# Mixer A's projection: moving operand in storage order, result permuted when it is split

## The chip, the cores and the metric

The kernel runs on one core of one Trainium2 chip. The metric is the device time of one execution in microseconds; lower is better. The engines are named as in the profile: PE (matrix multiply; PEld is its weight load), DVE (vector), ACT (scalar), POOL (GpSimd), SP (which here only issues DMAs). ACTq and POOLq are the queues on which ACT and POOL issue DMAs of their own.

## The reference

One decoder layer on 2048 tokens of width 1024. Cut to what matters here:

```python
h = rmsnorm(x, g_attn[l])
proj = jnp.einsum('bsd,de->bse', h, w_in[l]) + b_in[l]
qa, ka, va, qb, kb, vb = jnp.split(proj, splits, axis=-1)
oa = sliding_window_sink_gqa(qa, ka, va, sinks[l])   # Mixer A: rotary positions on q and k, window 128
ob = dilated_mixture(qb, kb, vb, rel_table)          # Mixer B: three dilated branches, T5 bias
mixed = jnp.concatenate([rmsnorm(oa, g_out_a[l]), rmsnorm(ob, g_out_b[l])], axis=-1)
x = x + jnp.einsum('bse,ed->bsd', mixed, w_o[l])
h = rmsnorm(x, g_ffn[l])
act = jax.nn.silu(h @ w_gate[l]) * (h @ w_up[l])
x = x + act @ w_down[l]
return rmsnorm(x, g_final)
```

Mixer A has 8 query heads and 2 key heads of 64 columns, so 512 + 128 columns of queries and keys; Mixer B has 8 and 8.

## The kernel before

Every fp32 product is made of three matmuls on operands split into a high and a low part (hh, hl for the normalised input, wh, wl for the weights). The input is held transposed: 128 partitions of the 1024 features in KC = 8 groups, by 2048 tokens (S). The tokens are stored by residue, token mod 16 first, in the order that the dilated branches of Mixer B want; four token tiles (t, NT = 4) of 512 columns make up the whole. Mixer A's attention wants another order, in which a block of 128 consecutive tokens lies together; in storage that is runs of 8 columns.

`project` has three stages. The first (to 148 us of the profiled execution) normalises x, transposes it into hh and hl and makes both mixers' values (`v_rows`). The second (148 to 280) makes Mixer A's queries and keys: five chunks c of 128 columns (0 to 3 queries, 4 keys), each with four tiles. `gemm(ps, w, t, True)` makes one tile of 24 matmuls of 128x512, whose moving operand is a view of hh or hl in Mixer A's order:

```python
mv = h[:, k, :].rearrange("p (r jj j a) -> p jj j r a", r=16, jj=4, j=4)[:, t]
```

A tile is then evicted with its rotary turn: DVE (L305) and ACT (L303) copy quarters with the halves exchanged, taking turns; DVE multiplies with cosine and sine (L307, L308); POOL adds (L309); ACT casts the high part (L311), DVE subtracts for the low part (L312), into a tile hia; SP stores it for two heads (`store_heads`, L185, 2 x 256 KB). The same stage makes Mixer B's bias tables, a step per tile: `rows(h)` multiplies a one-hot matrix to bias rows (accb), copies them out of the accumulator on ACT (lt) and stores them to a scratch Ls; `table(h)` loads them back skewed (tt, n4, n1), puts two parts in another order on DVE (L395, L396) and stores the table (Ts). Accumulators are eight.

The third stage (280 to 548) interleaves Mixer B's queries and keys (`proj_b`, 32 units of 24 matmuls with a contiguous moving operand, hi evicted by ACT L333 and DVE L334) with Mixer A's attention, `MixerA.unit`, which loads ka, va and qa (L534, L538, L542) on SP. Four B units come ahead of the first attention unit. `attend_b` follows; its first loads are q0 (L610) and the k tiles (L615).

A scheduler orders the instructions of each engine from this program; each engine then runs its own list in order and waits on semaphores. So what stands in an engine's queue behind a waiting instruction waits too, on SP and POOL as well.

Of the kernel before, what the change touches and what calls it, by code (L numbers as in the profile page):

```python
# [43 lines left out]
def shape_constants():  # L44
# [105 lines left out]
def project(tc, es, ident, half, x, g_attn, w_in, b_in, sinks, rel, rope, mask_a, onehot, sc):  # L150
# [19 lines left out]
    def gemm(ps, w, t, natural, tag="mm"):  # L170
        acc = ps.tile([P, 512], F32, tag=tag, name="acc")
        n = 0
        for k in range(KC):
            for a, h in ((w[0], hh), (w[0], hl), (w[1], hh)):
                if natural:
                    mv = h[:, k, :].rearrange("p (r jj j a) -> p jj j r a", r=16, jj=4, j=4)[:, t]
                else:
# [1 line left out]
                nc.tensor.matmul(acc, a[:, k, :], mv, start=(n == 0), stop=(n == 3 * KC - 1))  # L179
                n += 1  # L180
        return acc

    def store_heads(dst, h, hi, cols):
        for u in range(2):
            nc.sync.dma_start(dst[h + u].rearrange("s d n -> d s n")[:, :, cols], hi[u * 64:u * 64 + 64].bitcast(F32))  # L185
# [96 lines left out]
    with ExitStack() as ex:  # L282
        ps = ex.enter_context(tc.tile_pool(name="ps2", bufs=8, space=PSUM, reuse_waits="tile"))
        rp = ex.enter_context(tc.tile_pool(name="r1", bufs=2, reuse_waits="tile"))
# [9 lines left out]
        for c in range(5):  # L294
            w = load_w(c * P)
            for t in range(NT):
                cols = slice(t * 512, (t + 1) * 512)
                acc = gemm(ps, w, t, True)
                t1 = rp.tile([P, 512], F32, tag="t1", name="t1")
                for q4 in range(4):  # L300
                    d, s4 = t1[q4 * 32:(q4 + 1) * 32, :], acc[(q4 ^ 1) * 32:((q4 ^ 1) + 1) * 32, :]
                    if q4 % 2:
                        nc.scalar.copy(d, s4)  # L303
                    else:
                        nc.vector.tensor_copy(d, s4)  # L305
                t2 = rp.tile([P, 512], F32, tag="t2", name="t2")
                nc.vector.scalar_tensor_tensor(t2, acc, bcol[:, c:c + 1], tab[:, 0, cols], op0=ALU.add, op1=ALU.mult)  # L307
                nc.vector.scalar_tensor_tensor(t1, t1, bsw[:, c:c + 1], tab[:, 1, cols], op0=ALU.add, op1=ALU.mult)  # L308
                nc.gpsimd.tensor_add(t2, t2, t1)  # L309
                hi = rp.tile([P, 2, 512], F32R, tag="hi", name="hia")  # L310
                nc.scalar.copy(hi[:, 0], t2)  # L311
                nc.vector.tensor_sub(hi[:, 1], t2, hi[:, 0].bitcast(F32))  # L312
                store_heads(sc.qA if c < 4 else sc.kA, 2 * c if c < 4 else 0, hi, cols)
                n = c * NT + t - 2
                if 0 <= n < 2 * NH:
                    bias(n // NH, n % NH)
# [33 lines left out]
def bias_tables(tc, es, ps, rel, onehot, sc):  # L350
# [26 lines left out]
    def rows(h):  # L377
        lw = bw.tile([P, P], F32R, tag="lw", name="lw")
        nc.vector.tensor_scalar(out=lw, in0=ones, scalar1=rhi[:, h:h + 1].bitcast(F32), scalar2=None, op0=ALU.mult)
        lt = bw.tile([P, 3, 384], F32, tag="lt", name="lt")  # L380
        for b in range(3):
            acc = ps.tile([P, 384], F32, tag="mm", name="accb")
            nc.tensor.matmul(acc, lw, ohr[:, b, :], start=True, stop=True)
            nc.scalar.copy(lt[:, b, :], acc)
        nc.sync.dma_start(sc.L[h].rearrange("b p n -> p b n"), lt)

    def table(h):
# [7 lines left out]
        nc.vector.tensor_copy(tt[:, 128:384].rearrange("p (c i) -> p c i", c=4), n4.rearrange("p (i c) -> p c i", c=4))  # L395
        nc.vector.tensor_copy(tt[:, 384:640].rearrange("p (g c a) -> p g c a", g=4, c=4),  # L396
# [939 lines left out]
```

## Time and profile before

| | |
|---|---|
| median of 3 runs | 2397.68 us (2393.30 to 2399.03) |
| the profiled execution | 2399.05 us, its span 2397.3 us |
| mean granted TensorE clock | 0.98 |
| busy, share of the span | PE 96%, PEld 82%, DVE 67%, ACT 44%, POOL 21% |
| Mixer A's projection on PE | 147.8 to 279.8 us, 480 matmuls of 128x512 |
| B's projection and Mixer A's attention | 279.8 to about 548 us |

The rows in the prediction read: start or count, engine, line, operation, result<-operands by the program's names, shapes; behind a bar the busy time, the mean of one in ns, and the idle time ahead of it with what ended it.

### The profile page before, as it was taken

To read this page: it belongs to the slowest core of one execution; us is meant where nothing else is said; L and a number is where in the kernel's file an instruction comes from. 1 tells how busy PE (TensorE), PEld (TensorE's weight loads), DVE (VectorE), ACT (ScalarE), POOL (GpSimd) and SP (SyncE) were. 2 spreads that over 40 slices of the span, in tenths; PEclk is the share of its full clock that TensorE was granted. 3 is DMA by queue.
4 is the path that set the end of the run, shared out by engine and by line. 5 is a ranking of instruction groups with operands and counts; after the bars stand their busy time and mean duration, and the time that the engine had idled before them with its cause. 6 is when DMAs were issued, how large, how long until landed. Compare 5 with 4: busy or idle time off the path is not lost.

```text
span 2397.3 us, 34036 instructions
## 1 busy us (share of the span) xinstructions
PE 2302.2 (96%) x11765; PEld 1954.8 (82%) x11765; DVE 1608.9 (67%) x3155; ACT 1062.1 (44%) x2371; POOL 494.1 (21%) x447
## 2 busy tenths in 40 slices
PE   7999999997999979997999999899999999999998
PEld 7987788886999968885888888678888878888887
DVE  5435655456999986668877777787676747557555
ACT  5323355553988883434332323342333324444443
POOL 3211200001333220113233232423232330000000
PEclk9999999997999979998999999999999999999999
DMA  7666655559788566744554445333232339668663
GB/s 216 210 187 214 159 163 163 146 140 229 197 197 202 137 203 215 251 149 167 181 175 145 163 154 170 120 124 114 95 113 93 104 126 366 206 198 283 205 195 126
DMA packets 279228, 419.43 MB, mean 175 GB/s; under 512 B 24096, under 2 KB 152624, under 8 KB 274448
## 3 DMA queue, kind: packets, MB, share of 16 engines
q1 hardware_dynamic: 273072, 393.97, 53.9%
q10 hardware_dynamic: 3744, 17.11, 1.8%
q0 software_dynamic: 2240, 6.18, 1.0%
q8 instruction: 93, 1.52, 0.3%
q14 instruction: 79, 0.65, 0.1%
HBM read 278.11 MB, written 139.07 MB: 174 GB/s over the span
## 4 chain that ended last, share of the span: by engine, by line
PE 74%; DVE 11%; DMA 6%; ACT 4%; issue 3%; SPq 1%; POOL 1%; DVEq 0%; POOLq 0%; ACTq 0%
PE bY L1264 7%; PE acco L897 7%; PE Yu L1070 7%; PE acc L179 7%; PE Yg L1070 6%; PE bZ L1264 5%; PE bX L1264 5%; PE Zu L1070 5%; PE Xu L1070 4%; PE Zg L1070 4%; PE Xg L1070 4%; PE accv L246 4%; PE s L434 3%; DVE t L438 2%; PE pt L475 2%
## 5 line engine op out<-in xcount | busy, mean ns | idle before, releaser
L1217 DVE TENSOR_TENSOR o<-r,o 128x1024 fp32r<-128x1024 f32 x154 | 191.7, 1253 | 139.1 <-ACT o L1216 136.6
L1216 ACT CAST o<-r 128x1024 fp32r<-128x1024 f32 x154 | 161.3, 1050 | 227.9 <-PE bY L1264 84.0
L1164 POOL TENSOR_TENSOR c<-c,c 128x512 f32<-128x512 f32 x66 | 103.9, 1575 | 571.3 <-DVE c L1088 391.2
L1035 ACT CAST wh<-T 128x512 fp32r<-128x512 f32 x176 | 108.0, 623 | 248.1 <-PE Yu L1070 76.8
L456 ACT ACTIVATE p<-t,m 128x256 f32<-128x256 f32 (+1 forms) x384 | 179.0, 490 | 19.9 <-DVE m L682 19.7
L1264 PE MATMUL bY<-o 128*128 128x512 f32 x792 | 180.5, 389 | 0.0
L1264 PEld LDWEIGHTS bY<-o 128*128 128x128 f32 x792 | 148.6, 188 | 30.9
L179 PE MATMUL acc<-hh,wh 128*128 128x512 f32 x416 | 170.1, 409 | 0.7 <-DVE vt L249 0.7
L179 PE MATMUL acc<-hl,wh 128*128 128x512 f32 x416 | 170.2, 409 | 0.0
L179 PE MATMUL acc<-hh,wl 128*128 128x512 f32 x416 | 170.2, 409 | 0.0
L897 PE MATMUL acco<-woh,oT 128*128 128x512 f32 x512 | 164.0, 395 | 0.0
L481 DVE TENSOR_TENSOR hl<-pt,hl 128x512 fp32r<-128x512 f32 (+1 forms) x224 | 145.1, 657 | 22.0 <-ACT hl L480 21.5
L1037 DVE TENSOR_TENSOR wl<-T,wh 128x512 fp32r<-128x512 f32 x176 | 156.7, 901 | 0.4
L499 PE MATMUL o<-hl,v 128*128 128x128 f32 (+1 forms) x816 | 142.4, 299 | 10.6 <-DVE hl L481 7.4
L480 ACT CAST hl<-pt 128x512 fp32r<-128x512 f32 (+1 forms) x224 | 126.8, 574 | 38.8 <-PE pt L475 38.0
L475 PE MATMUL pt<-ident,p 128*128 128x128 f32 x848 | 135.5, 285 | 6.4 <-DVE hl L481 2.6
L434 PE MATMUL s<-k,q 128*128 128x256 f32 (+1 forms) x768 | 125.0, 299 | 16.6 <-DVE hl L481 6.2
L499 PEld LDWEIGHTS o<-hl,v 128*128 128x128 f32 x816 | 114.7, 200 | 14.4 <-DVE hl L481 9.8
L434 PEld LDWEIGHTS s<-k,q 128*128 128x128 f32 x768 | 106.0, 202 | 22.9 <-DVE hl L481 6.3
L1264 PE MATMUL bX<-o 128*128 128x512 f32 x528 | 120.6, 389 | 1.1 <-DVE o L1217 1.1
L1264 PE MATMUL bZ<-o 128*128 128x512 f32 x528 | 120.3, 389 | 0.0
L438 DVE CUSTOM_DVE_ANT_0 t<-s,tab 128x256 f32<-128x256 f32 (+1 forms) x344 | 112.6, 370 | 7.4 <-PE s L434 4.8
(470 smaller groups left out, 5817.4 us busy)
## 6 DMA issues: line engine op xcount, KB each, us to landing
r<-actS SPq DMA_DIRECT2D x154, 256.0 KB
actS<-c SPq DMA_DIRECT2D x128, 256.0 KB
wraw_g<-in_w_gate_dram SPq DMA_DIRECT2D x44, 512.0 KB
wraw_u<-in_w_up_dram SPq DMA_DIRECT2D x44, 512.0 KB
r<-wT SPq DMA_DIRECT2D x88, 256.0 KB
r<-in_w_down_dram SPq DMA_DIRECT2D x66, 256.0 KB
k<-kB SPq DMA_DIRECT2D x32, 512.0 KB
draw<-in_w_down_dram SPq DMA_DIRECT2D x22, 512.0 KB
```

The lines of the kernel that those rows point to most:

```text
L179: nc.tensor.matmul(acc, a[:, k, :], mv, start=(n == 0), stop=(n == 3 * KC - 1))
L434: nc.tensor.matmul(s[:, i, :n], b["q"], b["k"][m], start=(m == 0), stop=(m == 1))
L438: nc.vector.tensor_tensor_reduce(out=b["kv"](t[:, i, :n]), in0=b["kv"](s[:, i, :n]), in1=b["tab"], scale=-0.125, scalar=init, op0=ALU.add, ...
L456: nc.scalar.activation(b["pv"](p[:, i, :n]), b["tv"](b["t"]), AF.Exp, scale=-1.0, bias=nm[:, c:c + 1], accum_out=l[:, c:c + 1])
L475: nc.tensor.transpose(pt[:, sl, :], p[:, i, hfn * P:(hfn + 1) * P], ident)
L499: nc.tensor.matmul(out, v[:, vi, :], mov, start=(first and n == 1), stop=(last and n == 2 * len(jobs)))
L897: nc.tensor.matmul(acc, oT[t, g][kk // 2][:, kk % 2, a, i * P:(i + 1) * P], b[:, kk, :], start=(n == 0), stop=(n == 11))
L1037: nc.vector.tensor_sub(lo, src, hi.bitcast(F32))
L1070: nc.tensor.matmul(bank, a[:, k], b[:, k], start=(first and m == 0), stop=(m == 11), skip_group_check=not first)
L1216: nc.scalar.copy(o[:, 0], r)
L1217: V.tensor_sub(o[:, 1], r, o[:, 0].bitcast(F32))
L1264: nc.tensor.matmul(bank[i], o[:, u, 0, i * P:(i + 1) * P], o[:, v, 1, :], start=(first and j == 0 and m == 0), stop=(j == NP - 1 and m == ...
```

## The change

- hh and hl become four tiles each, one per token tile, and `gemm` reads the columns as they lie. The rope table's columns are put into the same order (in its host-made constant).
- Mixer A's result is brought into its order later: `rotated` evicts a tile up to the addition, `parted` casts and subtracts with writes in runs of 8 into one hia tile for a whole chunk, up to three tiles later, and stores 2 x 1 MB per chunk.
- The chunks run in the order 4, 0, 1, 2, 3; weights are loaded three tiles ahead, B's first weights before the stage ends.
- The bias tables go in finer steps: two of the 24 row pieces per tile, each with a store of its own; loads and the table's two copies on alternating tiles; the copies run on POOL.
- `proj_b` runs chunk 3 tile by tile, alternating queries and keys, and issues that chunk's 16 stores on ACT's queue.

The core of the diff (lines left out are the same edit at other places):

```diff
-    tok = (n // 128) * 128 + (n % 8) * 16 + res[(n % 128) // 8]
+    tok = (n % 128) * 16 + res[n // 128]
...
-    hh = cp.tile([P, KC, S], F32R, name="hh")
-    hl = cp.tile([P, KC, S], F32R, name="hl")
+    hh, hl = [], []
+    for t in range(NT):
+        hh.append(cp.tile([P, KC, 512], F32R, name=f"hh{t}"))
+        hl.append(cp.tile([P, KC, 512], F32R, name=f"hl{t}"))
...
-    def gemm(ps, w, t, natural, tag="mm"):
-                if natural:
-                    mv = h[:, k, :].rearrange("p (r jj j a) -> p jj j r a", r=16, jj=4, j=4)[:, t]
-                else:
-                    mv = h[:, k, t * 512:(t + 1) * 512]
-                nc.tensor.matmul(acc, a[:, k, :], mv, start=(n == 0), stop=(n == 3 * KC - 1))
+                nc.tensor.matmul(acc, a[:, k, :], h[t][:, k, :], start=(n == 0), stop=(n == 3 * KC - 1))
...
+    def store_heads(dst, h, hi, cols, q=nc.sync):
-            nc.sync.dma_start(dst[h + u].rearrange("s d n -> d s n")[:, :, cols], hi[u * 64:u * 64 + 64].bitcast(F32))
+            q.dma_start(dst[h + u].rearrange("s d n -> d s n")[:, :, cols], hi[u * 64:u * 64 + 64].bitcast(F32))
...
-        for c in range(5):
-            w = load_w(c * P)
...
+        rp = ex.enter_context(tc.tile_pool(name="r1", bufs=2, reuse_waits="tile"))
+        def rotated(c, t, w):
+            cols = slice(t * 512, (t + 1) * 512)
+            acc = gemm(ps, w, t)
...
+            t2 = rp.tile([P, 512], F32, tag="t2", name="t2", bufs=4)
...
+            nc.gpsimd.tensor_add(t2, t2, t1)
+            return t2.rearrange("p (r j a) -> p r j a", r=4, j=16)
+        def parted(c, t, t2):
+            if t == 0:
+                his[c] = rp.tile([P, 2, S], F32R, tag="hi", name="hia", bufs=1)
+            hi = his[c]
+            hj = [hi[:, u].rearrange("p (j r a) -> p r j a", j=16, r=16)[:, 4 * t:4 * t + 4] for u in range(2)]
+            tc.keep_in_program_order(nc.scalar.copy(hj[0], t2))
+            tc.keep_in_program_order(nc.vector.tensor_sub(hj[1], t2, hj[0].bitcast(F32)))
+            if t == NT - 1:
+                store_heads(sc.qA if c < 4 else sc.kA, 2 * c if c < 4 else 0, hi, slice(0, S))
+        his, behind, w = {}, [], {}
+        seq = [(c, t) for c in (4, 0, 1, 2, 3) for t in range(NT)]
+        w[4] = load_w(4 * P)
+        for n, (c, t) in enumerate(seq):
+            t2 = rotated(c, t, w[c])
+            if t == 1 and n + 3 < len(seq):
+                cn = seq[n + 3][0]
+                w[cn] = load_w(cn * P)
+            elif t == 1:
+                w_next = load_w(C_QB)
+            behind.append((c, t, t2))
+            if t in (0, 3):
+                for x_ in [x_ for x_ in behind if x_[1] in ((2, 3) if t == 0 else (0, 1))]:
+                    parted(*x_)
+                    del behind[[y[:2] for y in behind].index(x_[:2])]
+            if n >= 2:
+                bias(n - 2)
+        for x_ in behind:
+            parted(*x_)
...
+        w = {C_QB: w_next}
...
-                if t == 0:
-                    w = load_w(c0 + c * P)
+                if t == 0 and (c0, c) != (C_QB, 0):
+                    w[c0] = load_w(c0 + c * P)
...
-        units = [(c0, c, t) for c in range(4) for c0 in (C_QB, C_KB) for t in range(NT)]
+                store_heads(sc.kB if c0 == C_KB else sc.qB, 2 * c, hi, slice(t * 512, (t + 1) * 512),
+                            nc.scalar if c == 3 else nc.sync)
+        units = [(c0, c, t) for c in range(3) for c0 in (C_QB, C_KB) for t in range(NT)]
+        units += [(c0, 3, t) for t in range(NT) for c0 in (C_QB, C_KB)]
...
     def rows(h):
-        lt = bw.tile([P, 3, 384], F32, tag="lt", name="lt")
-        for b in range(3):
-            acc = ps.tile([P, 384], F32, tag="mm", name="accb")
-            nc.tensor.matmul(acc, lw, ohr[:, b, :], start=True, stop=True)
-            nc.scalar.copy(lt[:, b, :], acc)
-        nc.sync.dma_start(sc.L[h].rearrange("b p n -> p b n"), lt)
-    def table(h):
+        return lw
+    def piece(h, b):
+        if b == 0:
+            lws[h] = rows(h)
+        acc = ps.tile([P, 384], F32, tag="mm", name="accb")
+        nc.tensor.matmul(acc, lws[h], ohr[:, b, :], start=True, stop=True)
+        lt = bw.tile([P, 384], F32, tag="lt", name="lt")
+        nc.scalar.copy(lt, acc)
+        nc.sync.dma_start(sc.L[h, b], lt)
+    def load(h):
...
+        raws[h] = tt, n4, n1
+    def table(h):
+        tt, n4, n1 = raws[h]
+        nc.gpsimd.tensor_copy(tt[:, 128:384].rearrange("p (c i) -> p c i", c=4), n4.rearrange("p (i c) -> p c i", c=4))
+        nc.gpsimd.tensor_copy(tt[:, 384:640].rearrange("p (g c a) -> p g c a", g=4, c=4),
                               n1.rearrange("p (a c g) -> p g c a", g=4, c=4))
         nc.sync.dma_start(sc.T[h], tt)
+    def bias(step):
+        for n in (2 * step, 2 * step + 1):
+            if n < 3 * NH:
+                piece(n // 3, n % 3)
+        if step >= 2:
+            (table if step % 2 else load)(step // 2 - 1)
```

Where instructions move. SP's queue on the way into Mixer A's attention, before: kA's last stores, then the loads of ka, then B's first stores.

```order
L542 DMA qa_2808<-qA_60 128x2x512 [waits DMAHW1_49,DVE_49]
L542 DMA qa_2910<-qA_60 128x2x512 [waits DMAHW2_49]
L185 DMA kA_61<-hia_2626 64x2x512 [waits DMAHW3_49,DVE_49]
L185 DMA kA_61<-hia_2626 64x2x512 [waits DMAHW4_49]
L508 DMA mska_2645<-in_mask_a_dram 128x256 [waits DMAHW7_49,DMAHW5_49,DMAHW0_49]
L510 DMA snk_2647<-in_sinks_dram 128x8 [waits DMAHW6_49]
L534 DMA ka0_2800<-kA_61 64x512 [waits DMAHW4_49,DMAHW3_49]
L534 DMA ka0_2800<-kA_61 64x512
L534 DMA ka1_2803<-kA_61 64x512 [waits DMAHW1_49]
L534 DMA ka1_2803<-kA_61 64x512 [waits DMAHW2_49]
L185 DMA qB_62<-hi_2705 64x2x512 [waits DVE_49]
```

The same place after the change (hia_2616 is chunk 3, the last query chunk):

```order
L552 DMA mska_2644<-in_mask_a_dram 128x256 [waits DMAHW3_49,DVE_49]
L554 DMA snk_2646<-in_sinks_dram 128x8 [waits DMAHW4_49]
L578 DMA ka0_2793<-kA_61 64x512 x2
L578 DMA ka1_2796<-kA_61 64x512 [waits DMAHW7_49]
L183 DMA qA_60<-hia_2616 64x2x2048 [waits DMAHW0_49,DVE_49]
L183 DMA qA_60<-hia_2616 64x2x2048 [waits DMAHW1_49]
L578 DMA ka1_2796<-kA_61 64x512 [waits DMAHW2_49]
L582 DMA va_2799<-vA_64 128x4x128 [waits DMAHW3_49,PE_49]
L183 DMA qB_62<-hi_2698 64x2x512 [waits DMAHW4_49,DVE_49]
L183 DMA qB_62<-hi_2698 64x2x512 [waits DMAHW5_49]
L586 DMA qa_2801<-qA_60 128x2x512 [waits DMAHW6_49]
L586 DMA qa_2903<-qA_60 128x2x512 [waits DMAHW7_49]
```

The loads of ka stand ahead of the last stores of qA, and the loads of qa behind them, behind va and behind unit 0's stores.

The bias tables' copies, before, on DVE among the evictions (n is n4 or n1, t is t1 or t2):

```order
L379 TENSOR_SCALAR lw<-ones,rhi 128x128
L396 COPY tt<-n_2227 128x256
L312 TENSOR_TENSOR hia<-t_1845,hia 128x512
L305 COPY t_1892<-acc 32x512
L307 SCALAR_TENSOR_TENSOR t_1897<-acc,bcol,tab 128x512
L308 SCALAR_TENSOR_TENSOR t_1892<-t_1892,bsw,tab 128x512
L395 COPY tt<-n_2282 128x256
L305 COPY t_1944<-acc 32x512
L379 TENSOR_SCALAR lw<-ones,rhi 128x128
L305 COPY t_1944<-acc 32x512
L396 COPY tt<-n_2284 128x256
L312 TENSOR_TENSOR hia<-t_1897,hia 128x512
```

After the change they are on POOL, among the additions of the rotary turn:

```order
L305 TENSOR_TENSOR t2_1834<-t2_1834,t1_1829 128x512 [waits DVE_49,Activation_49]
L430 COPY tt_1964<-n1_1968 128x256 [waits DMAHW5_49,DMAHW6_49,DMAHW1_49,DMAHW0_49]
L305 TENSOR_TENSOR t2_1893<-t2_1893,t1_1888 128x512 [waits DVE_49,Activation_49]
L305 TENSOR_TENSOR t2_1948<-t2_1948,t1_1943 128x512 [waits DVE_49,Activation_49]
L429 COPY tt_2077<-n4_2079 128x256 [waits DMAHW6_49,DMAHW7_49,DMAHW0_49,Pool_49]
L430 COPY tt_2077<-n1_2081 128x256 [waits DMAHW4_49,DMAHW5_49,DMAHW3_49,DMAHW0_49]
L305 TENSOR_TENSOR t2_2003<-t2_2003,t1_1998 128x512 [waits DVE_49,Activation_49]
L429 COPY tt_2185<-n4_2187 128x256 [waits DMAHW3_49,DMAHW2_49,Pool_49]
L305 TENSOR_TENSOR t2_2055<-t2_2055,t1_2050 128x512 [waits DVE_49,Activation_49]
L430 COPY tt_2185<-n1_2189 128x256 [waits DMAHW2_49,DMAHW4_49,DMAHW1_49,DMAHW0_49]
```

L395 and L396 have left DVE, and L429 and L430 stand in POOL's queue with additions behind them.

SP's queue into attend_b, before and then after:

```order
L534 DMA ka_5199<-kA 64x640 x2
L542 DMA qa<-qA 128x2x512
L185 DMA kB<-hi 64x2x512 x2
L538 DMA va<-vA 128x5x128
L185 DMA kB<-hi 64x2x512 x2
L610 DMA q_5505<-qB 128x2048
L615 DMA k_0_5507<-kB 64x2048 x2
L615 DMA k_0_5510<-kB 64x2048 x2
```

```order
L586 DMA qa<-qA 128x2x512
L578 DMA ka_5189<-kA 64x640 x2
L578 DMA ka_5192<-kA 64x640 x2
L586 DMA qa<-qA 128x2x512
L582 DMA va<-vA 128x5x128
L654 DMA q_5498<-qB 128x2048
L659 DMA k_0_5500<-kB 64x2048 x2
L659 DMA k_0_5503<-kB 64x2048 x2
```

The stores of B's last chunk are gone from SP ahead of q0. They stand on ACT now, among the casts and exponentials of the attention:

```order
L355 ACTIVATE hi<-acc,bcol 128x512
L608 COPY rawa<-oa 64x512
L524 CAST hl<-pt_5048 128x512
L183 DMA kB<-hi 64x2x512
L524 CAST hl<-pt_5055 128x512
L183 DMA kB<-hi 64x2x512
L500 ACTIVATE p,la<-t,nma 128x256 x4
L355 ACTIVATE hi<-acc,bcol 128x512
L524 CAST hl<-pt_5131 128x512
L183 DMA qB<-hi 64x2x512
L608 COPY rawa<-oa 64x512
```

Each of these stores stands a few rows behind the ACTIVATE L355 whose unit it stores.

More of the change, by code (lines that the diff above doesn't have):

```diff
@@ L168, in load_w, with gemm @@
         return wh, wl
-    def gemm(ps, w, t, natural, tag="mm"):
+    def gemm(ps, w, t, tag="mm"):
         acc = ps.tile([P, 512], F32, tag=tag, name="acc")
@@ L245, in v_rows @@
                 for h, b in ((hh, w[0]), (hh, w[1]), (hl, w[0])):
-                    nc.tensor.matmul(acc, h[:, k, r * P:(r + 1) * P], b[:, k, :], start=(n == 0), stop=(n == 3 * KC - 1))
+                    nc.tensor.matmul(acc, h[r // 4][:, k, (r % 4) * P:(r % 4 + 1) * P], b[:, k, :], start=(n == 0), stop=(n == 3 * KC - 1))
                     n += 1
@@ L293, in project @@
         bias = bias_tables(tc, ex, ps, rel, onehot, sc)
-        for c in range(5):
-            w = load_w(c * P)
[L296 to L316, printed above, removed]
@@ new lines, in project @@
+        rp = ex.enter_context(tc.tile_pool(name="r1", bufs=2, reuse_waits="tile"))
+        def rotated(c, t, w):
+            cols = slice(t * 512, (t + 1) * 512)
+            acc = gemm(ps, w, t)
+            t1 = rp.tile([P, 512], F32, tag="t1", name="t1")
+            for q4 in range(4):
+                d, s4 = t1[q4 * 32:(q4 + 1) * 32, :], acc[(q4 ^ 1) * 32:((q4 ^ 1) + 1) * 32, :]
+                if q4 % 2:
+                    nc.scalar.copy(d, s4)
+                else:
+                    nc.vector.tensor_copy(d, s4)
+            t2 = rp.tile([P, 512], F32, tag="t2", name="t2", bufs=4)
+            nc.vector.scalar_tensor_tensor(t2, acc, bcol[:, c:c + 1], tab[:, 0, cols], op0=ALU.add, op1=ALU.mult)
+            nc.vector.scalar_tensor_tensor(t1, t1, bsw[:, c:c + 1], tab[:, 1, cols], op0=ALU.add, op1=ALU.mult)
+            nc.gpsimd.tensor_add(t2, t2, t1)
+            return t2.rearrange("p (r j a) -> p r j a", r=4, j=16)
@@ L394, in table @@
             nc.sync.dma_start(n1[g * 32:(g + 1) * 32], skew(h, 2, [(4, 4), (16, 8)], 127 + (W - 1) * g, 2 * P))
-        nc.vector.tensor_copy(tt[:, 128:384].rearrange("p (c i) -> p c i", c=4), n4.rearrange("p (i c) -> p c i", c=4))
-        nc.vector.tensor_copy(tt[:, 384:640].rearrange("p (g c a) -> p g c a", g=4, c=4),
+        raws[h] = tt, n4, n1
[3 more added lines that the diff above has]
+        nc.gpsimd.tensor_copy(tt[:, 384:640].rearrange("p (g c a) -> p g c a", g=4, c=4),
                               n1.rearrange("p (a c g) -> p g c a", g=4, c=4))
         nc.sync.dma_start(sc.T[h], tt)
-    return lambda step, h: (rows, table)[step](h)
+    lws, raws = {}, {}
+    def bias(step):
[4 more added lines that the diff above has]
+            (table if step % 2 else load)(step // 2 - 1)
+    return bias
 ident_f = lambda ap: ap
```

11 lines of the change are left out of this document (3 added, 8 removed).

## The prediction

> **What bounds the kernel now.** I read the page first (who is busy, what the chain that ended last is made of), then PE by stage, then the rows of the stage that the change rewrites, then what its neighbours wait for.
>
> ```profile
> span 2397.3 us, 34036 instructions
> PE 2302.2 (96%) x11765; PEld 1954.8 (82%) x11765; DVE 1608.9 (67%) x3155; ACT 1062.1 (44%) x2371; POOL 494.1 (21%) x447
> PE 74%; DVE 11%; DMA 6%; ACT 4%; issue 3%; SPq 1%; POOL 1%; DVEq 0%; POOLq 0%; ACTq 0%
> ```
>
> PE bounds the whole, so time comes out of this kernel where PE gets shorter or idles less. The windows show busy time of PE, PEld, DVE, ACT, POOL, then granted clock, DMA share, GB/s. The first is Mixer A's projection, the second B's just behind it, the third B's mixed with Mixer A's attention:
>
> ```profile
> 270.00:280.00 10.00, 10.00 (x39) 7.39 (x38) 7.07 (x11) 3.57 (x6) 2.56 (x2) 1.00 0.49 108
> 280.00:290.00 10.00, 10.00 (x45) 8.26 (x44) 6.72 (x10) 4.58 (x7) 4.12 (x2) 1.00 0.48 129
> ...
> 480.00:540.00 60.00, 60.00 (x354) 52.46 (x353) 31.68 (x88) 31.59 (x84) 4.35 (x7) 1.00 0.51 139
> ```
>
> PE is full in all three, at the full clock, with the same DMA share on both sides of 280; yet ten microseconds hold 39 matmuls before it and 45 behind it. Both are 128x512 matmuls of line L179 with 24 per tile. Line L179 in Mixer A's stage (148 to 280), then in B's (285 to 301); min/median/max ns:
>
> ```profile
> L179 PE MATMUL acc<-hh,wh x160: 417/428/512, 147.8 to 279.3; 128*128 128x512 f32 x160
> L179 PEld LDWEIGHTS acc<-hl,wh x160: 187/194/197, 147.9 to 279.3; 128*128 128x128 f32 x160
> ...
> L179 PE MATMUL acc<-hh,wh x24: 389/389/389, 284.8 to 300.5; 128*128 128x512 f32 x24
> L179 PEld LDWEIGHTS acc<-hl,wh x24: 187/188/188, 284.8 to 300.5; 128*128 128x128 f32 x24
> ```
>
> 428 ns against 389: the one difference in code is the moving operand, read in runs of 8 floats in the first and contiguously in the second. Matmuls overlap, so the price is the distance between starts, read from PE's timeline (start, duration):
>
> ```profile
> 148.13 0.42 PE L179 MATMUL acc<-hl,wh 128*128 128x512 f32 x1
> ...
> 151.80 0.44 PE L179 MATMUL acc<-hh,wh 128*128 128x512 f32 x1
> ...
> 299.34 0.39 PE L179 MATMUL acc<-hl,wh 128*128 128x512 f32 x1
> ...
> 301.61 0.39 PE L179 MATMUL acc<-hh,wl 128*128 128x512 f32 x1
> ```
>
> The first pair is 14 starts apart: 3.67/14 = 0.262 us. The second is 10 apart: 2.27/10 = 0.227 us.
>
> **The change, part by part.**
>
> *1. Contiguous moving operand.* 3 x 160 = 480 matmuls leave the 0.262 pace for 0.227: 480 x 0.035 = 16.8 us less. That lies on the path: PE has no idle time there to swallow it, and none behind it until 301. Ends: 0 (the pace doesn't come from the runs, a rival below) and 16.8. Taken: **-16.8**, since the operand becomes that of the 389 ns rows.
>
> *2. The work that must now keep up.* A tile gets 24 x 0.227 = 5.4 us of PE, in place of 6.3, and with its share of the bias rows about 5.7. What each group did in 148 to 280 (busy us, mean ns, idle before it):
>
> ```profile
> L305 DVE COPY t<-acc 32x512 f32<-32x512 f32 x36 | 24.8, 689 | 10.6 <-ACT t L303 5.1 <-PE acc L179 4.8
> L309 POOL TENSOR_TENSOR t<-t,t 128x512 f32<-128x512 f32 x17 | 23.4, 1375 | 103.3 <-DVE t L308 103.3
> L307 DVE SCALAR_TENSOR_TENSOR t<-acc,bcol,tab 128x512 f32<-128x512 f32 x18 | 13.5, 751 | 4.7 <-ACT t L303 4.3
> L308 DVE SCALAR_TENSOR_TENSOR t<-t,bsw,tab 128x512 f32<-128x512 f32 x18 | 13.4, 743 | 0.0
> L312 DVE TENSOR_TENSOR hia<-t,hia 128x512 fp32r<-128x512 f32 x17 | 11.7, 689 | 6.3 <-ACT hia L311 6.1
> ...
> L167 DVE TENSOR_TENSOR wl<-raw,wh 128x1024 fp32r<-128x1024 f32 x4 | 4.8, 1206 | 0.0
> L396 DVE COPY tt<-n 128x256 f32<-128x256 f32 x8 | 3.5, 440 | 10.0 <-DMA n<-Ls 9.7 <-issue 0.3
> L395 DVE COPY tt<-n 128x256 f32<-128x256 f32 x8 | 3.2, 397 | 16.0 <-DMA n<-Ls 8.8 <-DMA Ts<-tt 7.2
> ```
>
> DVE needs 2 x 0.689 + 0.751 + 0.743 + 0.689 = 3.56 us a tile plus a weight split (1.21) every fourth: 3.9 of 5.7. Moving L395 and L396 to POOL frees DVE of 6.7 us of copying and, more, of 25.7 us in which it stood before them for a DMA with evictions queued behind. The split by pairs writes runs of 8 rather than 512; the nearest rows with broken-up patterns are those copies (1.55 to 1.72 ns an element against 1.35 for L312), so at most 0.37 x 512 = 0.19 us a tile, hidden under PE while DVE has 1.8 us to spare. The single hia tile is refilled three tiles after its store is issued, 17 us for 2 MB; hidden too. Without waits the old chain ran at this pace (POOL's adds):
>
> ```profile
> 253.27 1.28 POOL L309 TENSOR_TENSOR t<-t,t 128x512 f32<-128x512 f32 x1 [3.30 <-DVE t L308]
> 257.55 1.29 POOL L309 TENSOR_TENSOR t<-t,t 128x512 f32<-128x512 f32 x1 [2.99 <-DVE t L308]
> 263.16 2.82 POOL L309 TENSOR_TENSOR t<-t,t 128x512 f32<-128x512 f32 x1 [4.33 <-DVE t L308]
> 270.32 1.28 POOL L309 TENSOR_TENSOR t<-t,t 128x512 f32<-128x512 f32 x1 [4.33 <-DVE t L308]
> ```
>
> 4.28 us between adds, 5.6 with a wait on ACT, 7.2 where a weight split falls in (the add beside it takes 2.82). Four tiles: 3 x 4.28 + 7.16 = 20.0, or 21.3 with one 5.6, against 4 x 5.7 = 22.8 of PE. PE stays the bound, by 7 to 12%.
>
> POOL now runs 16 table copies in order with its adds. POOL's price for them is in no row; from DVE's 0.40 us up to the dearest POOL instruction, 2.83; I take half an add, 0.64, since they have half its elements. POOL's sum is then 20 x 1.375 + 16 x 0.64 = 38 of 115 us. But an add behind a copy whose load is late waits with it. How fast tables can follow each other shows in the stores of the eight:
>
> ```profile
> L398 SPq DMA_DIRECT2D Ts<-tt x8: 320/362/1207, 183.7 to 250.5; - x8
> ...
> PE accb L383 <- DVE ohr L369: 1.0, 1, 1.0
> PE accb L383 <- DVE t L307: 0.5, 1, 0.5
> ```
>
> (250.5 - 183.7)/7 = 9.5 us a table, and that was bound by the chain load, copy, store (the waits on n<-Ls and Ts<-tt above). The new order gives a table two tiles, 11.4 us. It fits, with 1.9 us over; four t2 buffers and eight accumulators take up one late load. Where that cover is gone, PE stands. In the last two rows PE lost 1.5 us of the stage to bias rows already. Ends: 0, and the 16.8 eaten up to half where every table is late by a microsecond (8.4). Taken: **+1.5**, near the rows of idle PE that there are. The weights come three tiles ahead and w_next before the stage ends; their 1.21 us on DVE is counted above.
>
> *3. Into MixerA.* Order now: SP's stores and loads, then PE's first idle times behind the stage, then the throughput of a stretch in which the queue was full with large packets:
>
> ```profile
> 294.35 1.23 SPq L185 DMA_DIRECT2D kA<-hia  x2
> ...
> 299.37 2.44 SPq L534 DMA_DIRECT2D ka<-kA  x4
> ...
> 303.20 0.33 PE L434 MATMUL s<-ka,qa 128*128 128x128 f32 x1 [1.21 <-DMA ka<-kA]
> 304.54 1.08 PE L434 MATMUL s<-ka,qa 128*128 128x128 f32 x7 [1.01 <-DMA ka<-kA]
> 312.49 0.33 PE L475 MATMUL pt<-ident,p 128*128 128x128 f32 x1 [1.93 <-ACT p L456]
> ...
> DMA packets 159, 1.15 MB, mean 287 GB/s; under 512 B 19, under 2 KB 19, under 8 KB 19
> ```
>
> With chunk 4 first, kA is stored long before: the 2.2 us on ka<-kA go. Next late: qa. Its loads now stand on SP behind the last two qA stores (2 MB), va and unit 0's qB stores. Let T be the stage's end on PE. The last eviction (copies 2.6, two DVE steps 1.5, add 1.3, cast and subtract 1.3) ends at about T+7 to T+9; 2 MB at 287 GB/s are 7.3 us, qB's 0.5 MB and one qa 3.5 us more: qa lands at T+18 to T+22. Four B units, 96 x 0.227 = 21.8 us, cover that, barely; MixerA needs qa at T+21.8. If the evictions lag 5 us more, PE waits 5 us. Ends: -4.2 (all three idle times go) and +5 less the 2.2. Taken: **-1**, half of what waits on ka.
>
> *4. B's chunk 3.* Its 8 units are reordered and the 16 stores go to ACT's queue. ACT's price for issuing, from its only two DMAs, and SP's own:
>
> ```profile
> 0.73 0.45 ACTq L274 DMA_DIRECT2D brow<-in_b_in_dram  x1
> ...
> 547.68 1.23 SPq L185 DMA_DIRECT2D kB<-hi  x2
> 549.00 0.64 SPq L610 DMA_DIRECT2D q<-qB  x1
> ...
> 552.75 14.83 DMA k<-kB
> ```
>
> 16 x 0.45 to 0.62 us = 7 to 10 us of ACT over the last 50, where it is busy 31.6 of 60 and PE full: hidden, except that each store makes ACT stand for DVE's low half with exponentials queued behind. Ends 0 to 4 (16 x 0.25). Taken: **+0.5**, nearer 0 as there are gemm matmuls between.
>
> *5. attend_b's first loads.* SP's q0 issue followed two kB stores, 549.00 - 547.68 = 1.3 us, and the k loads that follow it end the wait of 14.83 us in the chain. Without those stores q0 goes 1.3 us sooner; it still has to wait for the last unit's eviction on DVE. Ends 0 and -1.3. Taken: **-1.3**.
>
> Sum: -16.8 + 1.5 - 1 + 0.5 - 1.3 = -17.1. The profiled execution took 2399.05 us (span 2397.3 and 1.8 around it), 1.4 above the runs' median of 2397.68; so 2381.9 on its scale, **2380.5** on the median's.
>
> **Rivals.**
> *A. The runs of 8 are not what slows PE.* For it: PEld's median is 194 ns in the slow stage and 188 in the fast one, and its operand is contiguous in both, so something may slow PE as a whole. Against it: the pace turns exactly at the stage's edge with clock and DMA share unchanged. Then term 1 is 0 and about 2397.5 remains: no change. [...] Chance 0.06.
>
> *B. Evictions bind the stage.* The margin of 7 to 12% goes, through ACT and DVE waiting on each other or DVE's weight split running into POOL: four tiles take 24 to 25 us in place of 22.8, five times, so 6 to 11 us come back: 2387 to 2391. Chance 0.15.
>
> *C. qa late.* Chunk 3's evictions lag, and PE waits 5 to 8 us before MixerA in place of the 2.2: 2384 to 2387. Chance 0.10.
>
> *D. Slower: the tables on POOL.* If copies or loads make a table take longer than its two tiles, adds queue behind copies, t2 and then the accumulators fill, and PE runs at the tables' pace. The stage is then 4 tiles (22.8) + 8 tables + about 2, and equals the old 131.9 us at 13.4 us a table; slower by 0.3% needs 14.3 or more, against 9.5 measured. Copies at 2.83 each give 9.5 + 2 x 2.4 = 14.3, just there: about 2405. Chance 0.03.
>
> **How the numbers follow.** My forecast, -12 to -22 us (2376 to 2386), has 0.66. A has 0.06, B 0.15, C 0.10, D 0.03. The range runs from 2374 (terms 2 and 4 zero, all of MixerA's first waits gone: -16.8 - 4.2 - 1.3 = -22.3, and a spread between runs of 0.1%) to 2389.5, which takes in C and half of B and leaves out A and D. 0.3%, 7 us, is about what a measurement of this kernel can tell from no change: faster holds the forecast, C and most of B, 0.88; same holds A and B's tail, 0.09; slower is D, 0.03.
>
> **What would show it.** Right: line L179's matmuls at 389 ns from 148 on, 45 in ten microseconds, the stage ending near 263; POOL's table copies near 0.6 us with no add waiting over 4 us; no PE idle time over 1 us before the first s<-ka,qa; the first k matmul of attend_b 1 us earlier against the last B unit. Wrong: matmuls still at 428 (A); PE idle on t or acc inside the stage (B), with POOL's copies ahead of the waits (D); PE waiting for qa<-qA (C).

## The result: slower, and the profile after

The changed kernel takes 2411.35 us, median of 5 runs (2407.56 to 2415.09), against 2398.22 for the kernel before (5 runs, 2393.30 to 2403.14): a ratio of 1.0054, 95% interval 1.004 to 1.0069, so 13 us slower. I had forecast 2380.5, faster, with 0.03 for slower.

The page's first lines after the change; PE does as many matmuls as before, 4 us shorter in sum, in a span that is 12 us longer:

```profile
span 2409.5 us, 33984 instructions
PE 2297.9 (95%) x11765; PEld 1956.9 (81%) x11765; DVE 1623.3 (67%) x3139; ACT 1061.0 (44%) x2371; POOL 513.0 (21%) x463
```

Where the time went shows best by landmarks, the first start of a group of matmuls. These are the groups of Mixer A's logits, attend_b's logits, the output projection and the feed-forward part's second half, before and then after (min/median/max ns, then first and last start):

```profile
L434 PE MATMUL s<-ka,qa x256: 220/287/562, 303.2 to 552.0; 128*128 128x256 f32 x119, 128*128 128x128 f32 x9
L434 PE MATMUL s<-k,q x768: 221/282/582, 562.4 to 832.5; 128*128 128x128 f32 x104, 128*128 128x256 f32 x88
L897 PE MATMUL acco<-woh,oT x512: 387/389/772, 890.7 to 1088.3; 128*128 128x512 f32 x171
L1264 PE MATMUL bX<-o x528: 388/389/497, 1969.3 to 2269.7; 128*128 128x512 f32 x176
```

```profile
L478 PE MATMUL s<-ka,qa x256: 220/287/562, 307.3 to 555.6; 128*128 128x256 f32 x119, 128*128 128x128 f32 x9
L478 PE MATMUL s<-k,q x768: 221/282/583, 558.4 to 830.5; 128*128 128x128 f32 x104, 128*128 128x256 f32 x88
L941 PE MATMUL acco<-woh,oT x512: 387/389/775, 885.0 to 1090.1; 128*128 128x512 f32 x171
L1308 PE MATMUL bX<-o x528: 388/389/500, 1981.2 to 2281.6; 128*128 128x512 f32 x176
```

Read as differences: Mixer A's attention starts 4.1 us later (not 17 sooner), attend_b's logits 4.0 sooner, the output projection 5.7 sooner, and the second half of the feed-forward part 11.9 later. So two things happened. The rewritten stage gained nothing. And 17.6 us were lost between the last two landmarks, more than 600 us behind it, in code that the diff doesn't touch: some 6 in the output projection's first 20 us and some 12 in the feed-forward part.

*In the stage.* PE has the pace that was forecast, then it stands. Line L177 in 148 to 260, three windows, and PE's waits between 148 and 320 (total, times, longest):

```profile
L177 PE MATMUL acc<-hh,wh x145: 389/389/628, 147.9 to 259.7; 128*128 128x512 f32 x145
```

```profile
160.00:170.00 10.00, 10.00 (x46) 8.32 (x45) 7.84 (x16) 3.75 (x7) 2.58 (x2) 1.00 0.21 67
...
220.00:230.00 10.00, 3.58 (x16) 2.65 (x15) 4.70 (x7) 1.63 (x4) 1.33 (x1) 0.85 0.93 228
270.00:280.00 10.00, 1.50 (x6) 0.94 (x5) 6.82 (x10) 3.78 (x6) 2.28 (x2) 0.74 0.79 184
```

```profile
PE acc L177 <- DVE t L303: 8.5, 1, 8.5
PE accb L412 <- ACT lt L414: 6.5, 1, 6.5
PE s L478 <- DMA qa<-qA: 3.3, 1, 3.3
```

46 matmuls in ten microseconds where there were 39, at 389 ns; then 6.5 us in which a bias row waits for ACT, 8.5 us in which B's first unit waits for an accumulator that DVE has not read, and a granted clock of 0.85 and 0.74 in the two windows in which these waits fall. B's first unit starts at 279.2 us, before at 280.0.

*In the feed-forward part.* Windows from 1185 to 1590 us, before, then after:

```profile
1185.00:1590.00 405.00, 395.70 (x1714) 321.93 (x1713) 303.47 (x412) 133.55 (x231) 115.98 (x74) 0.99 0.45 152
```

```profile
1185.00:1590.00 405.00, 388.08 (x1658) 313.30 (x1657) 303.39 (x392) 130.41 (x223) 119.50 (x74) 0.98 0.44 147
```

56 matmuls fewer in the same time: at 0.227 us, 12.7 us. What waits there now, on PE and DVE (1185 to 1545 us):

```profile
PE Yg L1114 <- DVE u L1126: 6.4, 6, 4.0
...
DVE T L1096 <- DMA wraw_g<-in_w_gate_dram: 35.7, 9, 4.9
```

Before, PE had no wait of that kind there, and DVE stood for that load for less than half as long:

```profile
DVE T L1052 <- DMA wraw_g<-in_w_gate_dram: 15.7, 9, 2.6
```

Matched matmul by matmul with the kernel before, the changed one falls back 12.4 us between 1185 and 1580, and 7.2 of these at one place. DVE stands 4.9 us for the gate's weights, the addition that PE needs starts at 1244.2, PE waits 4.0 us for it, and the next twelve matmuls take 0.63 us in place of 0.39:

```profile
1233.95 0.69 DVE L1096 TENSOR_TENSOR T<-wraw_g,T 128x512 f32<-128x512 f32 x1 [4.94 <-DMA wraw_g<-in_w_gate_dram]
...
1244.20 0.68 DVE L1126 TENSOR_TENSOR u<-Yg,c 128x512 f32<-128x512 f32 x1
...
1244.94 0.80 PE L1114 MATMUL Yg<-S3h,wh 128*128 128x512 f32 x1 [4.01 <-DVE u L1126]
1245.53 0.63 PE L1114 MATMUL Yg<-S3h,wl 128*128 128x512 f32 x1
```

The code is the same, its order is not. PE's rows show a steady pattern in each, here a stretch of the gate products (g) and up products (u); a name is the accumulator (X, Y or Z), g or u, and which of seven products of twelve matmuls is added to it (A11 to S4). First before, then after:

```
XgA11 YgS2 YuA22 ZuS4 ZgS1 YgS3 XgA12
XgA11 YuA22 ZuS4 XgA11 YgS2 ZgS1 XgA12 XuA11 YgS3
```

The scheduler places the whole program, and what changed at 150 to 550 us made it fall into another rhythm here; the next run shows this for one of the edits.

### The profile page after: what moved, and what is told of

Same layout as the page of the kernel before. It is cut to its first block, busy times and chain, and to the rows that moved or that the text cites. A ratio compares the mean times of both kernels' runs of the same rounds, so it can differ in the third digit from the quotient of the medians.

```text
span 2409.5 us, 33984 instructions
## 1 busy us (share of the span) xinstructions
PE 2297.9 (95%) x11765; PEld 1956.9 (81%) x11765; DVE 1623.3 (67%) x3139; ACT 1061.0 (44%) x2371; POOL 513.0 (21%) x463
## 4 chain that ended last, share of the span: by engine, by line
PE 40%; DVE 5%; DMA 4%; issue 1%; POOL 0%; DVEq 0%; POOLq 0%; ACT 0%; SPq 0%
PE bY L1308 7%; PE Yg L1114 5%; PE Yu L1114 5%; PE bZ L1308 5%; PE bX L1308 5%; PE Zu L1114 3%; PE Xu L1114 3%; PE Zg L1114 3%; PE Xg L1114 3%; DVE wl L1081 2%; DMA wraw_g<-in_w_gate_dram 2%; DMA draw<-in_w_down_dram 1%; DMA wT<-draw 1%; DVE T L1104 0%; DMA hraw<-hT 0%
## 5 line engine op out<-in xcount | busy, mean ns | idle before, releaser
L177 PE MATMUL acc<-hh,wh 128*128 128x512 f32 x416 | 165.9, 399 | 9.2 <-DVE t L303 8.5
L177 PE MATMUL acc<-hl,wh 128*128 128x512 f32 x416 | 165.4, 398 | 0.0
L177 PE MATMUL acc<-hh,wl 128*128 128x512 f32 x416 | 165.0, 397 | 0.0
L543 PEld LDWEIGHTS o<-hl,v 128*128 128x128 f32 x816 | 113.6, 197 | 15.1 <-DVE hl L525 12.4
L1079 ACT CAST wh<-wraw_u 128x512 fp32r<-128x512 f32 x66 | 41.1, 622 | 183.4 <-PE Yu L1114 83.7
```

Of the source, the lines that this page charges most:

```text
L177: nc.tensor.matmul(acc, a[:, k, :], h[t][:, k, :], start=(n == 0), stop=(n == 3 * KC - 1))
L543: nc.tensor.matmul(out, v[:, vi, :], mov, start=(first and n == 1), stop=(last and n == 2 * len(jobs)))
L1079: nc.scalar.copy(hi, src)
```

## Experiments on the feed-forward part

**Chunk 3's stores alone.** The kernel before, with one edit (and the argument for the queue in `store_heads`), which by itself gives the feed-forward part the changed kernel's order of matmuls:

```diff
-                store_heads(sc.kB if c0 == C_KB else sc.qB, 2 * c, hi, slice(t * 512, (t + 1) * 512))
+                store_heads(sc.kB if c0 == C_KB else sc.qB, 2 * c, hi, slice(t * 512, (t + 1) * 512), nc.scalar if c == 3 else nc.sync)
```

> The kernel before with one edit: the 16 stores of B's chunk 3 are issued on ACT's queue. This edit alone gives the feed-forward part the same order of instructions on every engine as in the changed kernel. Theory (the changed kernel's 12 us in the feed-forward part come from its order): the stretch from 1135 to 1560 us gets 10 to 13 us longer, attend_b starts 1 to 5 us sooner, the whole is 2403 to 2410. Rival (those 12 us are chance, or come from the time or place at which the earlier stages end): the feed-forward part takes what it takes before, the whole is 2393 to 2398.

2408.05 us, ratio 1.0042 (1.0027 to 1.0057). Against the kernel before, matmul by matmul, its profiled execution is 7.2 us ahead at 1185 us (1.7 of these already at 148, long ahead of the edit) and 6.7 behind at 1580: 13.9 us lost in between. By the medians, one edit at 500 us costs 11 us net, none of it near the edit.

**The order, exchanged both ways.** Edges between PE's matmuls pin the first half's order to that of the other kernel. SP's queue follows to within two rows, DVE's except for some rows in its first column blocks.

```diff
+        for n, count in PE_ORDER:
+            i = at.get(n, 0)
+            ins = made[n][i:i + count]
+            at[n] = i + count
+            if last is not None:
+                tc.add_manual_dep(ins[0].ins, last.ins.name, mybir.DependencyInfo(
+                    mybir.DependencyClass.NoSync, mybir.DependencyReason.DATA), reason="order")
+            last = ins[-1]
```

PE_ORDER lists, product by product, how many of its matmuls the other kernel has in a row.

> The changed kernel, with edges between the matmuls of the feed-forward part's first half that give PE the order of the kernel before there (DVE's and SP's queues follow it but for three rows). Theory (the order costs 12 us there): the stretch from 1185 to 1580 us of PE's work takes 12 us less than in the changed kernel, and the whole is 2398 to 2401. Rival (the loss comes from where the earlier stages end, or from the chip): nothing changes, 2409 to 2413.

> The kernel before, with edges that give PE in the feed-forward part's first half the order of the changed kernel; nothing else is changed. Theory: 12 us slower, 2408 to 2412. Rival: 2396 to 2400.

The changed kernel with the old order: 2399.26 us, ratio 1.0011 (1.0002 to 1.002). The kernel before with the new order: 2407.01, ratio 1.0047 (1.0032 to 1.0062), 1 us under the range expected. The same windows, changed kernel with the old order and kernel before with the new one:

```profile
1185.00:1590.00 405.00, 394.38 (x1711) 320.82 (x1710) 305.18 (x414) 132.57 (x231) 118.84 (x75) 0.99 0.46 153
```

```profile
1185.00:1590.00 405.00, 385.89 (x1653) 310.99 (x1652) 303.11 (x391) 129.17 (x222) 119.39 (x74) 0.98 0.45 147
...
PE Yg L1073 <- DVE u L1085: 8.3, 8, 3.1
```

1711 and 1653 matmuls, as 1714 and 1658: these 12 us go with the order, whichever kernel has it. That is shown. Why the scheduler settles there is not; and that the late load is what makes this order slow is read from the waits, as no run moved that load.

**Chunk 3 back on SP.** The changed kernel, with one edit:

```diff
-                            nc.scalar if c == 3 else nc.sync)
+                            nc.sync)
```

> The changed kernel with B's chunk 3 stores back on SP. The feed-forward part gets a third order of instructions, neither that of before nor that of the changed kernel. Theory (order decides there): the stretch from 1135 to 1560 us differs from both by some us; attend_b starts 1 to 5 us later than in the changed kernel. By the theory the whole lies anywhere from 2400 to 2415. Rival (the loss there comes from the stores on ACT or from the earlier stages): the stretch takes the 425 us of before or the 437 of the changed kernel, to 1 us.

2412.25 us, ratio 1.0068 (1.0047 to 1.009). Its third order loses 11.5 us between 1185 and 1580, near the changed kernel's 12.4; so this run doesn't tell theory from rival, the two exchanges do. It also starts attend_b's first products no sooner than the kernel before and is 5 us behind it at 610 us, where the changed kernel is 3.8 ahead: those stores are worth keeping on ACT.

## Experiments on the stage

**The operand alone.** The kernel before, with one edit:

```diff
-                acc = gemm(ps, w, t, True)
+                acc = gemm(ps, w, t, False)
```

> The kernel before with one edit: Mixer A's 480 matmuls read their 512 columns as they lie (so its queries and keys come out in another order; all else, evictions, stores and bias tables, is as before, and the order of instructions on every engine is that of before). If the runs of 8 set the pace, the stage 148 to 280 us ends near 263 to 266 us and the whole gains 13 to 17 us: 2381 to 2385. If the old evictions with their bias tables on DVE (9.5 us a table, 18 us behind) can't follow the faster PE, PE idles in the stage and the gain is 3 to 10 us: 2388 to 2395. If the evictions cannot follow at all, no gain: 2398.

2397.19 us, ratio 1.0005 (0.9991 to 1.0019): nothing. PE runs at the new pace (389 ns) and waits 8.7 us in the stage for bias rows and accumulators; B's first unit starts at 271.1, 9 us sooner (1 of them from an earlier start of the stage). Then PE waits 7.6 us on ka<-kA, since the last evictions, which are kA's, come only 2.8 us sooner. This is the third outcome of the expectation, almost to the microsecond.

```profile
PE s L434 <- DMA ka<-kA: 7.6, 2, 6.7
PE accb L383 <- DVE t L307: 5.6, 3, 2.4
PE accb L383 <- DVE ohr L369: 2.5, 1, 2.5
```

The additions on POOL, one a tile, are the evictions' clock. First and last start (the columns behind the ns) of the kernel before, of it with the operand alone, and of the changed kernel:

```profile
L309 POOL TENSOR_TENSOR t<-t,t x20: 1272/1286/2831, 158.6 to 291.7; 128x512 f32<-128x512 f32 x20
```

```profile
L309 POOL TENSOR_TENSOR t<-t,t x20: 1263/1287/2835, 157.2 to 288.9; 128x512 f32<-128x512 f32 x20
```

```profile
L305 POOL TENSOR_TENSOR t<-t,t x20: 1262/1309/2975, 164.6 to 284.6; 128x512 f32<-128x512 f32 x20
```

(291.7 - 158.6)/19 = 7.0 us a tile before, when PE needed 6.6, and still 6.9 with the operand alone; 6.3 after the change, when PE needs 5.7. So the evictions bound this stage already, behind a cover of eight accumulators. The mean hides two stretches: in the kernel before, the first thirteen additions (158.6 to 253.3) came every 7.9 us, while the bias tables were made, and the last eight, behind the last table's store at 250.5, every 5.5. What holds them, in the changed kernel (ACT, then POOL):

```profile
ACT lt L414 <- DMA Ls<-lt: 21.5, 7, 6.6
...
POOL tt L429 <- DMA Ts<-tt: 23.6, 5, 8.9
POOL tt L429 <- DMA n<-Ls: 13.7, 2, 9.2
POOL tt L430 <- DMA n<-Ls: 9.7, 5, 4.0
```

ACT stands for a free lt buffer, with the evictions' quarter copies behind it; POOL stands for tables' loads and stores for 47 us, with the additions behind it. (The first addition is also 6 us later than before, as DVE waits 5.4 us ahead of it for the load of the relative-position table; the kernel without transfers below has that too, at 164.3, so it isn't what binds.)

**The 2 MB stores.** The first suspicion was the burst of two 1 MB stores per chunk, ahead of the rows' stores: on another queue (first edit), or cut in four over three tiles (second edit).

```diff
-                store_heads(sc.qA if c < 4 else sc.kA, 2 * c if c < 4 else 0, hi, slice(0, S))
+                store_heads(sc.qA if c < 4 else sc.kA, 2 * c if c < 4 else 0, hi, slice(0, S), nc.scalar)
...
+                late.extend((dst[h0 + u, s], hi[u * 64:u * 64 + 64, s].bitcast(F32)) for s in range(2) for u in range(2))
...
+            for dst, src in late[:2 if t == 2 else 1]:
+                tc.keep_in_program_order(nc.sync.dma_start(dst, src))
```

> The changed kernel with one edit: the ten 1 MB stores of Mixer A's chunks go to ACT's queue, so that the bias rows' stores and loads on SP do not stand behind them; the orders of PE, DVE and of the feed-forward part stay. Theory (SP's queue is what PE waits for in the stage, through the bias rows' copies on ACT): the two idle times of PE (6.5 and 8.5 us) go, and the stage ends 13 to 20 us sooner; the whole is 2392 to 2399. Rival (the evictions on DVE, ACT and POOL are too slow for PE in themselves, or POOL's table copies hold the additions): the idle times stay, 2408 to 2413.

> The changed kernel, with each chunk's two 1 MB stores cut into four of 512 KB that are issued over three tiles. Theory (the 16 DMA engines are taken for 10 us by each 2 MB burst, whichever queue issued it; the bias rows' stores wait behind it, ACT waits for a free lt buffer, and the evictions wait behind ACT): shorter bursts halve ACT's waits for Ls<-lt of 6 to 11 us, PE's idle time in the stage falls from 15.6 us to under 8, the whole is 2398 to 2406. Rival (it is the sum of the stage's traffic or the evictions that is too slow, not the burst): idle time stays over 12 us, 2407 to 2413.

2408.4 (1.0047, 1.003 to 1.0063) and 2408.23 (1.0045, 1.0031 to 1.0059): the rivals hold. B's first unit starts at 278.1 and 282.2. Neither the queue nor the burst is the cause.

**Half the transfers, then all, then the work.** Rows stored for head 0 alone, from which all heads' tables are loaded; then loads for head 0 alone as well; then no bias tables in the stage at all. The eight tables' stores stay in all three, so most tables hold wrong values. The first edit below stands in the first two kernels (with `sc.L[0, b]` in the loads), the second in the second alone, the third in the third, which leaves out `bias_tables`.

```diff
-        nc.sync.dma_start(sc.L[h, b], lt)
+        if h == 0:
+            nc.sync.dma_start(sc.L[h, b], lt)
...
     def load(h):
+        if h:
+            raws[h] = raws[0]
+            return
...
-            if n >= 2:
-                bias(n - 2)
+            if n % 2 == 0 and 2 <= n <= 16:
+                nc.sync.dma_start(sc.T[n // 2 - 1], tab[:, 0, 0:640])
```

> The changed kernel, with the bias rows of heads 1 to 7 not stored, and all tables loaded from head 0's rows (the tables of seven heads are wrong by that; the matmuls, the copies on ACT, the loads and POOL's copies stay). Theory (lt's wait for its store is what stops ACT): no wait of ACT on Ls<-lt, PE idle in the stage under 2 us, the stage ends at 262 to 265 us; the feed-forward part keeps its 12 us, one run is 2387 to 2395. Rival (POOL's copies and loads, or the evictions, hold PE): PE's two idle times of 6 to 9 us stay, over 2404.

> The changed kernel with all of the bias tables' instructions on PE, ACT, DVE and POOL, but with the rows' stores and the tables' loads done for head 0 alone (the tables of the other seven heads are head 0's); the eight tables' stores stay. Theory (the evictions are late by what the queues of ACT and POOL wait for these transfers): additions every 5.5 to 5.9 us, PE's idle time ahead of B's first unit under 4 us, that unit starts at 261 to 268 us, the whole 2390 to 2398 with the feed-forward part's 12 us in it. Rival (it is the tables' own work on POOL, ACT and PE, not the transfers): additions every 6.2 us or more, B's first unit after 275.

> The changed kernel without the bias tables' work in Mixer A's stage (no rows, no loads, no copies on POOL; the eight tables are filled from the rope table, so their values are wrong; their eight stores stay). PE does 24 matmuls less there (4 us). Theory (the bias tables' transfers, through ACT's and POOL's queues, make the evictions take 6.3 us a tile, from the first addition to the last): the additions come every 5.3 to 5.7 us, PE's pace, PE has no idle time over 1.5 us at the stage's end, and B's first unit starts at 258 to 261 us, against 288 in the changed kernel. Rival 1 (the single hia tile and its 2 MB stores hold them): ACT waits over 8 us on qA<-hia, PE idles 4 us or more at the end. Rival 2 (DVE and ACT waiting for each other): additions every 6 us or more with no DMA wait.

The additions of the three, in this order:

```profile
L305 POOL TENSOR_TENSOR t<-t,t x20: 1260/1292/2970, 163.9 to 283.7; 128x512 f32<-128x512 f32 x20
```

```profile
L305 POOL TENSOR_TENSOR t<-t,t x20: 1277/1322/2977, 164.3 to 266.9; 128x512 f32<-128x512 f32 x20
```

```profile
L304 POOL TENSOR_TENSOR t<-t,t x20: 1282/1573/2830, 161.3 to 262.8; 128x512 f32<-128x512 f32 x20
```

Without the rows' stores the pace stays 6.3 us: ACT's wait for lt is gone, POOL's waits stay at 48 us, and PE's two idle times have become one of 17.8 us, behind which B's first unit starts at 278.3. My theory of lt alone fell.

```profile
POOL tt L431 <- DMA n<-Ls: 25.6, 7, 10.4
...
POOL tt L430 <- DMA Ts<-tt: 22.4, 6, 11.2
```

Without the rows' stores and the loads of seven heads, but with every copy, row and matmul, it is 5.4 us, and B's first unit starts at 261.5: 18.5 us sooner than before (17.7 from the stage's start), the 16.8 of the forecast and about 1 more. Without any tables, 5.3 us and 256.8 (24 matmuls fewer), a little under the 258 expected; the 288 given there for the changed kernel should be 279.2. So what binds the stage are these transfers of the bias tables: ACT and POOL wait for them with evictions behind. Which of the two directions costs how much, and how much of it is traffic that slows the other transfers, stays open, as no kernel left out the loads alone. A sum of waits is not the price, either: in the kernel at PE's pace, POOL still stands 22.9 us for the tables' stores.

```profile
POOL tt L433 <- DMA Ts<-tt: 22.9, 7, 8.5
```

The runs took 2401.27, 2391.16 and 2385.21 us (one each; the first in neither of the ranges expected), each with another order in the feed-forward part than the kernel before.

**Two hia tiles.** The kernel without tables, with these edits, and with three t2 buffers in place of four:

```diff
-                his[c] = rp.tile([P, 2, S], F32R, tag="hi", name="hia", bufs=1)
+                his[c] = rp.tile([P, 2, S], F32R, tag="hi", name="hia", bufs=2)
...
-            if t in (0, 3):
...
+            parted(*behind.pop())
```

> As the kernel without the bias tables' work, and with two hia tiles instead of one, each tile split at once instead of up to three tiles later. If the single hia tile holds the evictions there, its waits go and PE's idle time with them; if nothing held them, B's first unit starts where it does with one hia tile, to 1.5 us.

One run of 2384.07; B's first unit at 258.2, additions every 5.3 us. The single hia tile holds nothing there.

## A version that beats both

**The kernel before, chunk 3's stores on ACT, the feed-forward part's order kept.** The edit to `store_heads`' last argument and the edges, both as shown above:

> The kernel before with B's chunk 3 stores on ACT's queue, and edges that keep the feed-forward part's order of the kernel before. Theory: what the stores on ACT bring ahead of the feed-forward part stays (5 us at 1185 us), and its 14 us of loss go: 2390 to 2394. Rival (the gain of 5 us is chance between executions or is given back later): 2396 to 2400.

2393.09 us, ratio 0.9987 (0.9976 to 0.9998): 3 to 4 us faster than the kernel before, as expected, and by the two ratios some 16 faster than the changed one. In the profiled execution it is 7.2 us ahead at 1175 us and ends 8.0 ahead; that execution is the fastest of twelve, so it shows more than the medians do. The margin is small, and the interval only just leaves out 1.

## Why the prediction was wrong, step by step

- *Contiguous operand (-16.8).* The price was right: 389 ns, 46 in ten microseconds. That all of it lies on the path was wrong. The same instruction in the same stage has a median of 428 ns with its moving operand in runs of 8, and of 389 with the columns as they lie, and the kernel with the operand alone has the new pace too. So Rival A is out, though the whole came out no faster. By what mechanism the runs cost those 39 ns, no run shows.
- *The work that must keep up (+1.5).* The first step that failed. From PE's first matmul to B's first unit the stage took 132.2 us before and 131.4 after, so this term was about +15.9. I took the evictions' pace from four additions without waits (4.28 to 7.2 us) and the tables' from their stores (9.5 us against 11.4), each as if it ran alone. The four additions lie at 253 to 270 us, behind the last table; all twenty give 7.0 us a tile, more than PE's 6.6: the margin of "7 to 12%" was a deficit that the accumulators hid. And I counted the 25.7 us in which DVE stood before the copies as freed. They went with the copies, as 47 us, to POOL, through which every eviction passes too. The tables' stores now run from 179.2 to 268.6, 12.8 us a table, where 11.4 was the room. Rival B had evictions that bind, with the wrong cause (DVE and ACT waiting for each other) and too little, 6 to 11 us where 15.9 went. Rival D had the place, POOL's queue, and the mechanism, additions behind copies, but not the price: the copies took 0.63 to 1.09 us, about as assumed; what they wait for was late. That the whole came out slower, as D has it, is not D's doing, as the stage did not get longer.

```profile
L430 POOL COPY tt<-n x8: 629/702/1092, 178.6 to 267.6; 128x256 f32<-128x256 f32 x8
...
L316 DVE TENSOR_TENSOR hia<-t,hia x20: 678/898/1784, 176.0 to 287.6; 128x512 fp32r<-128x512 f32 x20
...
L315 DVE TENSOR_TENSOR hia<-t,hia x20: 679/688/1790, 174.7 to 265.7; 128x512 fp32r<-128x512 f32 x20
```

  The split in runs of 8, which I had priced at up to 0.88 us, has a median of 0.90 here, and of 0.69 in the kernel without tables (the last row), with the same pattern: the pattern costs nothing there, and what lengthens it goes with the tables.
- *Into MixerA (-1).* Rival C came true in kind, with 3.3 us where it had 5 to 8: PE waits on qa<-qA, the loads having been issued at 299.1 behind qB's stores. Without tables, where PE comes sooner, that wait is 7.4 us:

```profile
PE s L477 <- DMA qa<-qA: 7.4, 1, 7.4
```

- *Chunk 3 on ACT (+0.5).* Near nothing where it stands, as said: against the kernel before, PE is 0.7 us behind at 320 us and 1.1 at 545. But I left out that a store on another queue lets the scheduler order later work anew, and had no term for the feed-forward part, which is to put it at nothing. The order there is the program's, could be read ahead of the run like the rows that I quoted, and differs from the first column block on. This is the second step that failed, and it alone cost 12 us.
- *attend_b's first loads (-1.3).* Right in kind, too small. SP issues q0 at 546.9 and k at 547.3, before at 549.0 and 549.7, and the first k matmul comes 4.0 us sooner though the last of Mixer A's logits start 3.6 us later (555.6 and 552.0):

```profile
546.94 0.33 SPq L654 DMA_DIRECT2D q<-qB  x1
547.32 2.43 SPq L659 DMA_DIRECT2D k<-kB  x4
```

The balance: Mixer A's stage and its transition +0.7 us (by 320 us), attend_b's start -5, and another -2 at its end; the first 20 us of the output projection take 6 back, at a clock of 0.86 where it was 1.00; the feed-forward part +12.

```profile
900.00:910.00 10.00, 10.00 (x39) 8.06 (x40) 5.49 (x10) 2.51 (x4) 1.04 (x1) 0.86 1.04 359
```

By PE's rows, each of the eight kernels with chunk 3 on ACT and all matmuls loses 3 to 7 us there, and those with it on SP lose nothing. The eight had won 4 to 5 us just before: from 850 to 910 us together, the changed kernel loses 3.5 us and the others 0.7 to 2.2. No run was made on that; it stays open.

## What to carry to other kernels

Before pricing a faster engine, take the pace of what follows it over the whole stage, first to last, not from its best stretch: a lag hidden by a ring of buffers is not slack (here 7.0 us a tile against the 6.6 of PE, behind eight accumulators). In an engine's queue that runs in order, a copy that waits for a transfer holds everything behind it, on whichever engine it is put (DVE stood 25.7 us for the tables' transfers, POOL then 47); take the transfer away to find out, not the instruction. And where a scheduler orders the program, compare its order in every later stage, and price or pin what moved: here an edit at 500 us cost 12 to 14 us from 1200 on.

## What the runs showed that I had not expected

- An order of the same matmuls with the same operands is worth 12 to 14 us of 400 in the profiled executions, and 10 to 13 by the ratios of medians. Six to eight waits of PE on a DVE addition behind a late load are 6.4 to 8.3 us of that; matmuls at a lower granted clock behind the longest of them (0.50 from 1244.9 to 1250.0 us in the changed kernel) are, by my estimate from their 0.63 us in place of 0.39, some 2 to 4 more.
- In the changed kernel, PE's idle times of 8.5, 6.5 and 4.0 us were each followed by 4 to 6 us of slow matmuls (0.63 us in place of 0.39; the granted clock from 279.2 to 284.9 us is 0.50), so that 8.5 us of waiting cost near 11.
